# The MLP's second product as running PSUM sums over two pairs of output blocks, with the residual added by GpSimd's DMA in seven of eight groups

## The chip, the cores and the metric

One core of one Trainium2 chip. The metric is the device time of one execution in microseconds, the median of several runs; lower is better.

## The reference

Two residual layers over one sequence of 1024 positions, model width 1024, all in fp32. Layer 0 mixes tokens with a gated linear recurrence, layer 1 with causal attention ("fox"); beside each stands a cross-attention into 256 memory tokens ("kv" is its projection of the memory). Each layer ends in an MLP with squared ReLU:

```python
def sqrelu_mlp(h, w1, w2):
    return jnp.square(jax.nn.relu(h @ w1)) @ w2

for layer in range(DEPTH):            # DEPTH = 2
    h = rms_norm(x, norm_mix[layer])
    ...
    x = x + jnp.concatenate([y_mix, y_mem], axis=-1) @ w_out[layer]
    x = x + sqrelu_mlp(rms_norm(x, norm_mlp[layer]), w_mlp_in[layer], w_mlp_out[layer])
return x
```

`w_mlp_in` is 1024 x 4096, `w_mlp_out` 4096 x 1024.

## The kernel before

Activations stand transposed: 128 features on the partitions, 1024 positions in two halves of H = 512 columns. Each fp32 operand is split into a high and a low part in a rounded format (`r`, `wh`/`wl`), and a product is three matmuls (`t3`: high by high twice crossed with the low parts, summed in PSUM). The residual stream x lies in HBM as `xs` (the trace calls it xspill), in blocks of 128 features by 512 positions, 256 KB each.

The MLP (`mlp`) runs over eight groups g of four hidden blocks m = 4g to 4g+3. For each hidden block, `mlp_z` computes both halves of the first product, 24 matmuls for each into a bank of tag pj; VectorE takes the ReLU out of PSUM and GpSimd squares it. `hid_parts` makes the seven combinations of hidden blocks that a seven-product (Strassen-Winograd) 2x2 block multiplication needs, and splits them. `mlp_out` is the second product: 28 products of 6 matmuls, 168 per group. A group is 192 + 168 = 360 matmuls of 128x512, and the next group's first hidden block is computed ahead of the second product. The weights' own combinations are made by GpSimd in `_wsplit`, from raw loads into two `wraw` buffers.

In `mlp_out`, a step q works on a 2x2 group of blocks c11, c12, c21, c22: features 2q and 2q+1, both halves. Each of its seven products has its own PSUM bank. ScalarE copies the first out (L994), VectorE adds the others from PSUM into t, u or a residual block in SBUF (L995, L998, L1002, L1005, L1013, L1014, L1019, L1024: eight adds for each q), and GpSimd adds t and u into residual blocks (L1006, L1007, L1015). The four residual blocks are loaded by SyncE (`acc_load`, L449) and stored by it (`sink`, L980), in every group. In group 7 of layer 0, `sink` also adds the squares of the finished block to the sum for the next norm (`sqacc`, L398 to L407), and splits half 0's blocks as the next layer's input (L412, L413); the norm's matmuls (L341, into tag o, "pso") wait for the last of these sums. In group 7 of layer 1 it stores to the output.

The program is put in order by a scheduler that simulates the engines, so that instructions of neighbouring steps interleave on each engine; each engine then runs its own list in that order. SBUF blocks come from a pool of NU = 81 slots shared by all stages: a slot is written again when its earlier readers, DMAs among them, are done. PSUM has eight banks: two of tag pj, two of s, three of pt, one of o.

Of the kernel before, what the change touches and what calls it, by code (L numbers as in the profile page):

```python
# [19 lines left out]
P = 128  # L20
S = 1024
D = 1024
H = 512
# [133 lines left out]
class Builder:  # L157
    NU = 81
# [3 lines left out]
    def __init__(self, ctx, tc, ins, out):  # L162
# [13 lines left out]
        self.wraw = [cst.tile([P, 1056], F32, name=f"wr{i}") for i in range(2)]  # L176
# [23 lines left out]
        self.zz = {}  # L200
        self.xg = [None, None]
# [71 lines left out]
    def _wraw(self, upto):  # L273
        while self.wrawn < min(len(self.plan), upto):
            i = self.wrawn
            buf, src = self._wrawbuf(i), self.plan[i][0]
            n = 1024 if self.plan[i][2] == "s1" else self.plan[i][1]
# [9 lines left out]
    def _wsplit(self, upto):  # L287
        nc = self.nc
        while self.wload < min(len(self.plan), upto):
# [10 lines left out]
            elif parts in ("s1", "s2"):  # L300
                G, q = nc.gpsimd, 256
                a11, a12, a22, a21 = (raw[:, k * q:(k + 1) * q] for k in range(4))
                f = self.F.get()
                if parts == "s1":
                    self.wx = f
                    G.tensor_tensor(f[:, q:2 * q], a21, a22, ALU.add)  # L306
                    G.tensor_tensor(f[:, 0:q], f[:, q:2 * q], a11, ALU.subtract)  # L307
                    self._wpart(hi[:, 0:512], lo[:, 0:512], raw[:, 0:512], nc.vector)
                    self._wpart(hi[:, 512:1024], lo[:, 512:1024], f[:, 0:512], nc.vector)
                else:  # L310
                    G.tensor_tensor(f[:, 0:q], a11, a21, ALU.subtract)
                    G.tensor_tensor(f[:, q:2 * q], a12, self.wx[:, 0:q], ALU.subtract)
                    self._wpart(hi[:, 512:768], lo[:, 512:768], a22, nc.vector)
                    self._wpart(hi[:, 0:512], lo[:, 0:512], f[:, 0:512], nc.vector)
                    self.F.put(self.wx, f)
# [7 lines left out]
            self._wraw(self.wload + 2)  # L323

# [630 lines left out]
    def acc_load(self, q):  # L955
        return {(a, b): self.load_x(2 * q + a, b, self.xs) for a in range(2) for b in range(2)}

    def mlp_out(self, l, g, parts, acc):
        nc = self.nc
        V, G = nc.vector, nc.gpsimd  # L960
        n = slice(0, H)

        def prod(ps, blk, w, key):
            terms = []
            for p in range(2):
                c = slice(blk * M + p * P, blk * M + (p + 1) * P)
                terms += self.t3(w[0][:, c], w[1][:, c], *parts[p][key])
            for j, (a, b) in enumerate(terms):
                nc.tensor.matmul(ps, lhsT=a, rhs=b, start=(j == 0), stop=(j == 5))  # L969
            if q == 3:  # L970
                for p in range(2):
                    self.R.put(*parts[p][key])

        def sink(a, b):
            f = acc[(a, b)]
# [5 lines left out]
            if g == 7 and l == 0:  # L981
                self.sqacc(dm, b, x, V if b == 0 and a == 1 else None)
                if b == 0:
                    self.xg[0].append(self.split(x, self.pc("gmix1", dm)))
            self.F.put(f)

        for q in range(4):
            c11, c12, c21, c22 = (acc[(a, b)][:, n] for a in range(2) for b in range(2))
            w = self.wnext()
            tf, uf = self.F.get(), self.F.get()  # L990
            t, u = tf[:, n], uf[:, n]
            p1 = self.psum("pj")
            prod(p1, 0, w, "b11")
            nc.scalar.activation(t, p1, AF.Copy)  # L994
            V.tensor_tensor(c11, c11, p1, ALU.add)  # L995
            p2 = self.psum("pj")
            prod(p2, 1, w, "b21")
            V.tensor_tensor(c11, c11, p2, ALU.add)  # L998
            sink(0, 0)
            p6 = self.psum("pt")  # L1000
            prod(p6, 2, w, "t2")
            V.tensor_tensor(t, t, p6, ALU.add)  # L1002
            p5 = self.psum("s")
            prod(p5, 3, w, "t1")
            V.tensor_tensor(u, t, p5, ALU.add)  # L1005
            G.tensor_tensor(c12, c12, u, ALU.add)  # L1006
            G.tensor_tensor(c22, c22, u, ALU.add)  # L1007
            self.F.put(uf)
            nxt = self.acc_load(q + 1) if q < 3 else None
            w = self.wnext()  # L1010
            p7 = self.psum("s")
            prod(p7, 0, w, "t3")
            V.tensor_tensor(t, t, p7, ALU.add)  # L1013
            V.tensor_tensor(c22, c22, p7, ALU.add)  # L1014
            G.tensor_tensor(c21, c21, t, ALU.add)  # L1015
            self.F.put(tf)
            p3 = self.psum("pt")
            prod(p3, 1, w, "b22")
            V.tensor_tensor(c12, c12, p3, ALU.add)  # L1019
            sink(0, 1)  # L1020
            sink(1, 1)
            p4 = self.psum("pt")
            prod(p4, 2, w, "t4")
            V.tensor_tensor(c21, c21, p4, ALU.add)  # L1024
            sink(1, 0)
            acc = nxt

    def mlp(self, l, src, nz, nw, nxt=None):
# [11 lines left out]
        for g in range(8):  # L1040
# [6 lines left out]
            acc = self.acc_load(0)  # L1047
# [538 lines left out]
```

## Time and profile before

| | |
|---|---|
| median of 3 runs | 2181.33 us (2180.13 to 2185.57) |
| span of the profiled execution | 2182.0 us |
| mean granted TensorE clock | 0.992 |
| MLP of layer 0, steady groups | about 375 to 975 us |
| MLP of layer 1, steady groups | about 1650 to 2100 us |
| last matmul starts | 2175.14 us |

The engines are TensorE (PE), VectorE (DVE), ScalarE (ACT), GpSimd (POOL) and SyncE (SP), which issues most DMAs. A row of the groups of instructions reads: line, engine, operation, output tile, input tiles, shape, how often, busy us and mean ns of one, idle time before it and what ended that. "SPq" and "POOLq" are the queues of DMAs that SyncE and GpSimd issue.

### The profile page before, as it was taken

The numbers are of one execution on the slowest core, as the hardware profiler recorded it, in microseconds if no ns is written. First come the engines' busy times: TensorE is split into PE (matmuls) and PEld (weight loads), VectorE is DVE, ScalarE is ACT, GpSimd is POOL, SyncE is SP. The second block draws the span as 40 slices with busy tenths as digits, with TensorE's granted clock in tenths as the row PEclk, the third lists the DMA queues.
The fourth block names the chain that finished last, engine by engine and source line by source line (L and its number), as shares of the span: only waits on it lengthen the run. The fifth ranks groups of instructions, "written<-read, shape, count | busy, mean of one in ns | idle before, by whom it ended". The sixth has DMA issues, their size and how long they took to land. (4 is left out here: it accounts for less than half of the span.)

```text
span 2182.0 us, 31206 instructions
## 1 busy us (share of the span) xinstructions
PE 2124.3 (97%) x10662; PEld 1775.0 (81%) x10662; DVE 1621.9 (74%) x2942; ACT 906.4 (42%) x1776; POOL 944.4 (43%) x965
## 2 busy tenths in 40 slices
PE   8999999999999999998999999999999999999998
PEld 6898777888888888876999998776778888888887
DVE  8998685767767667779677778777887677677676
ACT  6755643232222222245555746656332322222322
POOL 3222312554544444448342324332555545545454
PEclk9999999999999999999999999999999999999999
DMA  5333253535435436444768446835365355354353
GB/s 184 126 88 90 90 189 108 178 115 174 157 116 191 145 112 202 136 154 155 262 243 288 139 145 204 280 91 152 114 214 177 109 163 163 119 182 147 114 191 132
DMA packets 152607, 345.71 MB, mean 158 GB/s; under 512 B 17088, under 2 KB 19200, under 8 KB 152448
## 3 DMA queue, kind: packets, MB, share of 16 engines
q1 hardware_dynamic: 143232, 318.49, 45.1%
q0 software_dynamic: 9216, 25.24, 3.8%
q8 instruction: 84, 1.38, 0.3%
q14 instruction: 75, 0.61, 0.1%
HBM read 237.65 MB, written 106.00 MB: 157 GB/s over the span
## 5 line engine op out<-in xcount | busy, mean ns | idle before, releaser
L348 PE MATMUL pspj<-r,wh 128*128 128x512 f32 x2576 | 818.6, 398 | 12.4 <-ACT wh L284 6.5
L348 PEld LDWEIGHTS pspj<-r,wh 128*128 128x128 f32 x2576 | 483.1, 189 | 125.1 <-ACT wh L284 6.9
L348 PE MATMUL pspj<-r,wl 128*128 128x512 f32 x1288 | 513.7, 399 | 2.0 <-DMA wl<-wsp 1.5
L284 ACT ACTIVATE wh<-wr 128x256 fp32r<-128x256 f32 (+3 forms) x417 | 242.5, 605 | 451.2 <-PE pspt L969 188.2
L285 DVE TENSOR_TENSOR wl<-wr,wh 128x256 fp32r<-128x256 f32 (+2 forms) x368 | 311.0, 853 | 85.2 <-ACT wh L284 84.4
L348 PEld LDWEIGHTS pspj<-r,wl 128*128 128x128 f32 x1288 | 245.9, 191 | 62.9 <-DMA wl<-wsp 2.8
L927 POOL TENSOR_TENSOR f<-f 128x512 f32<-128x512 f32 x128 | 153.5, 1199 | 325.3 <-DVE f L926 310.3
L348 PE MATMUL pspj<-wh,r 128*128 128x256 f32 (+1 forms) x1408 | 272.9, 288 | 8.0 <-ACT f L499 3.9
L418 ACT ACTIVATE r<-f 128x512 fp32r<-128x512 f32 x250 | 156.5, 630 | 293.3 <-POOL f L927 145.2
L421 DVE TENSOR_TENSOR r<-f,r 128x512 fp32r<-128x512 f32 x250 | 203.7, 826 | 74.0 <-ACT r L418 73.8
L969 PE MATMUL pspt<-r,wh 128*128 128x512 f32 x768 | 246.4, 395 | 1.0 <-DVE f L1019 1.0
L348 PEld LDWEIGHTS pspj<-wh,r 128*128 128x128 f32 x1408 | 223.8, 191 | 11.2 <-ACT f L499 4.4
L348 PE MATMUL pspj<-wl,r 128*128 128x256 f32 (+1 forms) x704 | 200.5, 285 | 0.9 <-DVE wl L285 0.9
L1006 POOL TENSOR_TENSOR f<-f,f 128x512 f32<-128x512 f32 x64 | 84.2, 1316 | 236.6 <-DVE f L1005 233.0
L969 PEld LDWEIGHTS pspt<-r,wh 128*128 128x128 f32 x768 | 143.7, 188 | 35.3 <-issue 2.1
L969 PE MATMUL pss<-r,wh 128*128 128x512 f32 x512 | 161.0, 395 | 3.6 <-ACT wh L284 2.7
L969 PE MATMUL pspj<-r,wh 128*128 128x512 f32 x512 | 160.1, 394 | 1.4 <-DVE f L995 1.4
L284 ACT ACTIVATE wh<-f 128x512 fp32r<-128x512 f32 x128 | 80.9, 632 | 180.5 <-PE pspj L969 76.5
L969 PE MATMUL pspt<-r,wl 128*128 128x512 f32 x384 | 151.8, 396 | 0.0
L926 DVE SCALAR_TENSOR_TENSOR f<-pspj,f 128x512 f32<-128x512 f32 x128 | 87.9, 688 | 77.2 <-PE pspj L348 72.8
L348 PEld LDWEIGHTS pspj<-wl,r 128*128 128x128 f32 x704 | 134.2, 191 | 2.3 <-DVE wl L285 1.3
L969 PEld LDWEIGHTS pss<-r,wh 128*128 128x128 f32 x512 | 95.9, 188 | 26.6 <-ACT wh L284 3.2
(279 smaller groups left out, 3647.7 us busy)
## 6 DMA issues: line engine op xcount, KB each, us to landing
f<-xspill SPq DMA_DIRECT2D x312, 256.0 KB, 3.3
xspill<-f SPq DMA_DIRECT2D x288, 256.0 KB, 3.3
wr<-in_w_dram SPq DMA_DIRECT2D x134, 512.0 KB, 3.9
f<-in_xT_dram SPq DMA_DIRECT2D x32, 256.0 KB, 3.9
wr<-in_wkv_dram SPq DMA_DIRECT2D x16, 512.0 KB, 3.7
wr<-in_wina_dram SPq DMA_DIRECT2D x15, 512.0 KB, 3.8
wsp<-wh SPq DMA_DIRECT2D x14, 512.0 KB, 4.5
wsp<-wl SPq DMA_DIRECT2D x14, 512.0 KB, 4.7
```

The source lines that it names most:

```text
L284: self.wact = self.nc.scalar.activation(hi, raw, AF.Copy)
L285: eng.tensor_tensor(lo, raw, hi.bitcast(F32), ALU.subtract)
L348: self.lastmm = self.nc.tensor.matmul(out, lhsT=a, rhs=b, start=(j == 0), stop=(j == n - 1))
L418: i = self.nc.scalar.activation(hi[:, :n], src, AF.Copy)
L421: self.nc.vector.tensor_tensor(lo[:, :n], src, hi[:, :n].bitcast(F32), ALU.subtract)
L926: nc.vector.scalar_tensor_tensor(r[:, n], ps, 0.0, self.rsb[h][:, n], ALU.max, ALU.mult)
L927: nc.gpsimd.tensor_tensor(r[:, n], r[:, n], r[:, n], ALU.mult)
L969: nc.tensor.matmul(ps, lhsT=a, rhs=b, start=(j == 0), stop=(j == 5))
L1006: G.tensor_tensor(c12, c12, u, ALU.add)
```

## The change

The second product is computed for two steps q at once (a pair u of q = 2u and 2u+1), in seven phases b11, b21, t2, t3, t1, t4, b22 of 2 x 6 matmuls. The products b11, t2, t1 and b22 are summed one after another in the same bank, one bank for each q of the pair: tag s for u = 0, tag pj for u = 1. ScalarE copies that running sum out after b11, after t2 and after t1. So a sum that VectorE or GpSimd formed from copies is now formed in PSUM by TensorE; the number of matmuls stays 168 in a group.

In groups 0 to 6 (`out_added`) no residual block is loaded: what a group adds to each block is made in an SBUF buffer, and GpSimd issues a DMA that adds it to the block in HBM (`send`, 16 in a group). Group 7 loads the blocks, adds to them in SBUF and stores them, since their values are needed for the norm or the output.

For this the weights come in another order, seven units of 1024 columns for a group; GpSimd combines them 512 columns at a time (L332 to L335), eight times in a group. There are three raw weight buffers in place of two, and two slots fewer in the pool.

```diff
-    NU = 81
+    NU = 79
...
-        self.wraw = [cst.tile([P, 1056], F32, name=f"wr{i}") for i in range(2)]
+        self.wraw = [cst.tile([P, 1056], F32, name=f"wr{i}") for i in range(3)]
...
+                    G.tensor_tensor(x["S3"][:, :512], a11, a21, ALU.subtract)
+                    G.tensor_tensor(x["S2"][:, :512], a22, x["S3"][:, :512], ALU.subtract)
+                    G.tensor_tensor(x["S1"][:, :512], a21, a22, ALU.add)
+                    G.tensor_tensor(x["S4"][:, :512], a12, x["S2"][:, :512], ALU.subtract)
...
-            for q in range(4):
-                self.plan += [(self.ins["w2"][(l * 8 + g) * 4 + q], 1024, "s1"), (None, 768, "s2")]
+            r = [self.ins["w2"][(l * 8 + g) * 4 + k] for k in range(4)]
+            self.plan += [(r[0], 1024, ("a11a12",)), (r[1], 1024, ("S2", "S3")), (None, 1024, ("S1", "a22")),
+                          (r[2], 1024, ("S4", "a11")), (r[3], 1024, ("a12", "S2")), (None, 1024, ("S3", "S1")),
+                          (None, 1024, ("a22", "S4"))]
...
     def mlp_out(self, l, g, parts, acc):
...
+        for u in range(2):
+            qs = (2 * u, 2 * u + 1)
+            ta, tc = ("s", "pt") if u == 0 else ("pj", "pt")
+            A = [self.psum(ta) for _ in qs]
...
+            def add_to(a, b, other=None):
+                def done(qq, q, ps):
+                    c = acc[(q, a, b)][:, n]
+                    V.tensor_tensor(c, c, ps, ALU.add)
+                    if other is not None:
+                        G.tensor_tensor(c, c, other[qq][:, n], ALU.add)
+                        self.F.put(other[qq])
+                        sink(q, a, b)
+                return done
+
+            if g < 7:
+                self.out_added(u, qs, A, t, t2, uu, phase, copy_to)
+                continue
...
+            phase(A, "b11", True, False, copy_to(t))
+            phase([self.psum(tc) for _ in qs], "b21", True, True, add_to(0, 0, t))
...
+            phase(A, "t2", False, False, copy_to(t2))
+            C = [self.psum(tc) for _ in qs]
+            phase(C, "t3", True, False, add_to(1, 1))
...
+            phase(A, "t1", False, False, mid)
...
+            phase(C, "t4", False, True, add_to(1, 0, t2))
...
+            phase(A, "b22", False, True, end)
+
+    def out_added(self, u, qs, A, t, t2, uu, phase, copy_to):
...
+        def send(f, q, a, b):
+            nc.gpsimd.dma_start(self.xs[2 * q + a, :, b * H:(b + 1) * H], f[:, n], accum_op=ALU.add)
+            self.F.put(f)
+
+        def plus(dst, a, b):
+            def done(qq, q, ps):
+                f = dst[qq][:, n]
+                V.tensor_tensor(f, f, ps, ALU.add)
+                if a is not None:
+                    send(dst[qq], q, a, b)
+            return done
+
+        phase(A, "b11", True, False, copy_to(t))
+        phase([self.psum("pt") for _ in qs], "b21", True, True, plus(t, 0, 0))
+        phase(A, "t2", False, False, copy_to(t2))
+        C = [self.psum("pt"), self.psum("o")]
+        phase(C, "t3", True, True, plus(t2, None, None))
...
+        phase(A, "t1", False, False, mid)
+        phase([self.psum("pt") for _ in qs], "t4", True, True, plus(t2, 1, 0))
...
+        phase(A, "b22", False, True, end)
```

Three places show how the order moves. First GpSimd's list in a steady group of layer 0, before; L306 to L312 combine weights (f is a slot, wr a raw buffer), L927 squares a hidden block, L1006 to L1015 add into the residual:

```order
L927 TENSOR_TENSOR f_479_4618<-f_479_4618 128x512
L311 TENSOR_TENSOR f_495_4765<-wr_72 128x256
L312 TENSOR_TENSOR f_495_4765<-wr_72,f_488_4711 128x256
L1006 TENSOR_TENSOR f_474_4552<-f_474_4552,f_482_4630 128x512
L1007 TENSOR_TENSOR f_476_4556<-f_476_4556,f_482_4630 128x512
L1015 TENSOR_TENSOR f_475_4554<-f_475_4554,f_481_4629 128x512
L306 TENSOR_TENSOR f_496_4801<-wr_71 128x256
L307 TENSOR_TENSOR f_496_4801<-f_496_4801,wr_71 128x256
L311 TENSOR_TENSOR f_503_4855<-wr_71 128x256
L312 TENSOR_TENSOR f_503_4855<-wr_71,f_496_4801 128x256
```

The same group in the change (L953 squares a hidden block, L1085 is the DMA that adds):

```order
L953 TENSOR_TENSOR f_449_4445<-f_449_4445 128x512
L335 TENSOR_TENSOR f_477_4631<-wr_73,f_475_4629 128x512
L334 TENSOR_TENSOR f_476_4630<-wr_71 128x512
L953 TENSOR_TENSOR f_468_4518<-f_468_4518 128x512
L953 TENSOR_TENSOR f_469_4546<-f_469_4546 128x512
L1085 DMA xspill<-f_470_4562 128x512
L1085 DMA xspill<-f_471_4570 128x512
L1085 DMA xspill<-f_472_4600 128x512
L1085 DMA xspill<-f_478_4644 128x512
L1085 DMA xspill<-f_473_4608 128x512
```

The combinations, which stood among the adds, now stand ahead of the second product among the squares; behind them stand the sixteen DMAs of the group, with no arithmetic between.

Second, VectorE's list at the end of layer 0's last group, before: adds from PSUM, low parts of weights (L285), splits of finished blocks (L413) and sums of squares (L407), which end with the sum that the norm waits for:

```order
L1005 TENSOR_TENSOR f_951_8908<-f_950_8907,pss_8942 128x512
L413 SCALAR_TENSOR_TENSOR r_954_8931<-f_940_8840,par,r_953_8930 128x512
L1024 TENSOR_TENSOR f_926_8734<-f_926_8734,pspt_8882 128x512
L407 TENSOR_TENSOR f_905_8597<-f_905_8597,f_947_8891 128x512
L413 SCALAR_TENSOR_TENSOR r_949_8895<-f_926_8734,par,r_948_8894 128x512
L285 TENSOR_TENSOR wl_77<-wr_71,wh_74 128x256
L1019 TENSOR_TENSOR f_941_8842<-f_941_8842,pspt_8971 128x512
L1013 TENSOR_TENSOR f_950_8907<-f_950_8907,pss_8961 128x512
```

And in the change (L1040 adds from PSUM, L286 makes low parts, L431 sums squares, L437 splits):

```order
L1040 TENSOR_TENSOR f_891_8372<-f_891_8372,pspt_8391 128x512
L387 SCALAR_TENSOR_TENSOR rmt_8700<-rmt_8700,vm_8697 128x2
L388 SCALAR_TENSOR_TENSOR rm_8699<-rmt_8700,rm_8699 128x2
L1040 TENSOR_TENSOR f_894_8415<-f_894_8415,pspj_8309 128x512
L286 TENSOR_TENSOR wl_79<-wr_73,wh_76 128x256
L1040 TENSOR_TENSOR f_895_8417<-f_895_8417,pspj_8310 128x512
L431 TENSOR_TENSOR f_850_8143<-f_850_8143,f_900_8463 128x512
L437 SCALAR_TENSOR_TENSOR r_902_8467<-f_890_8370,par,r_901_8466 128x512
L431 TENSOR_TENSOR f_850_8143<-f_850_8143,f_903_8479 128x512
```

Each q has four adds here where it had eight, the last four come as two pairs, and the small steps of the kv norm (L387, L388) stand among them.

Third, SyncE's list at the start of layer 1's MLP, before; L280 loads raw weights, L840 stores a residual block that the layer's output projection finished, L449 loads one and L980 stores one of the second product:

```order
L840 DMA xspill<-f_1640_15649 128x512
L280 DMA wr_72<-in_w_dram 128x1024
L840 DMA xspill<-f_1644_15676 128x512
L280 DMA wr_71<-in_w_dram 128x1024
...
L449 DMA f_1687_15990<-xspill 128x512
L980 DMA xspill<-f_1684_15984 128x512
L280 DMA wr_71<-in_w_dram 128x1024
L449 DMA f_1693_16073<-xspill 128x512
L980 DMA xspill<-f_1685_15986 128x512
```

In the change (L864 stores what the output projection finished, L281 loads raw weights):

```order
L864 DMA xspill<-f_1588_15154 128x512
L281 DMA wr_71<-in_w_dram 128x1024
L864 DMA xspill<-f_1592_15181 128x512
L281 DMA wr_72<-in_w_dram 128x1024
L281 DMA wr_73<-in_w_dram 128x1024
L281 DMA wr_71<-in_w_dram 128x1024
```

From the last store of the output projection on, only weight loads stand in the list until group 7.

More of the change, by code (lines that the diff above doesn't have):

```diff
@@ L299, in _wsplit @@
                     nc.gpsimd.dma_start(b, d[:, a:a + n])
[L300 to L315, printed above, removed]
+            elif isinstance(parts, tuple):
+                self._wunit(hi, lo, raw, parts)
             else:
@@ L961, in mlp_out, with prod, free, sink @@
         n = slice(0, H)
-        def prod(ps, blk, w, key):
+        seen = set()
+        def prod(ps, w, qq, key, start, last):
             terms = []
             for p in range(2):
-                c = slice(blk * M + p * P, blk * M + (p + 1) * P)
+                c = slice((qq * 2 + p) * P, (qq * 2 + p + 1) * P)
                 terms += self.t3(w[0][:, c], w[1][:, c], *parts[p][key])
             for j, (a, b) in enumerate(terms):
[L969 to L975, printed above, removed]
+                nc.tensor.matmul(ps, lhsT=a, rhs=b, start=(start and j == 0), stop=(j == 5), skip_group_check=not start)
+        def free(key):
+            for p in range(2):
+                self.R.put(*parts[p][key])
+        def sink(q, a, b):
+            f = acc.pop((q, a, b))
             x, dm = f[:, n], 2 * q + a
@@ L981, in sink @@
             if g == 7 and l == 0:
-                self.sqacc(dm, b, x, V if b == 0 and a == 1 else None)
+                self.sqacc(1 if b in seen else 0, b, x, V if b == 0 and a == 1 else None)
+                seen.add(b)
                 if b == 0:
-                    self.xg[0].append(self.split(x, self.pc("gmix1", dm)))
+                    self.xg[0][dm] = self.split(x, self.pc("gmix1", dm))
             self.F.put(f)
[L987 to L1026, printed above, removed]
@@ new lines, in mlp_out, with phase, copy_to, mid @@
+        for u in range(2):
+            qs = (2 * u, 2 * u + 1)
+            ta, tc = ("s", "pt") if u == 0 else ("pj", "pt")
+            A = [self.psum(ta) for _ in qs]
+            t, t2, uu = [None] * 2, [None] * 2, [None] * 2
+            def phase(banks, key, start, last, done):
+                w = self.wchunk()
+                for qq in range(2):
+                    prod(banks[qq], w, qq, key, start, last)
+                    done(qq, qs[qq], banks[qq])
+                if u == 1:
+                    free(key)
+            def copy_to(dst):
+                def done(qq, q, ps):
+                    dst[qq] = self.F.get()
+                    nc.scalar.activation(dst[qq][:, n], ps, AF.Copy)
+                return done
[11 more added lines that the diff above has]
+                continue
+            if u == 0:
+                self.acc_load(acc, u, 0, 0)
+            self.acc_load(acc, u, 1, 1)
+            phase(A, "b11", True, False, copy_to(t))
+            phase([self.psum(tc) for _ in qs], "b21", True, True, add_to(0, 0, t))
+            self.acc_load(acc, u, 1, 0)
+            phase(A, "t2", False, False, copy_to(t2))
+            C = [self.psum(tc) for _ in qs]
+            phase(C, "t3", True, False, add_to(1, 1))
+            self.acc_load(acc, u, 0, 1)
+            def mid(qq, q, ps):
+                copy_to(uu)(qq, q, ps)
+                c = acc[(q, 1, 1)][:, n]
+                G.tensor_tensor(c, c, uu[qq][:, n], ALU.add)
+                self.F.put(uu[qq])
+                sink(q, 1, 1)
+            phase(A, "t1", False, False, mid)
+            if u == 0:
+                self.acc_load(acc, 1, 0, 0)
+            phase(C, "t4", False, True, add_to(1, 0, t2))
+            def end(qq, q, ps):
+                add_to(0, 1)(qq, q, ps)
+                sink(q, 0, 1)
+            phase(A, "b22", False, True, end)
```

58 lines of the change are left out of this document (52 added, 6 removed).

## The prediction

> **What bounds the kernel now.** I read first the head of the page, then a table of busy time by stretch of 75 us, then the chain that ended last, then the waits of TensorE in the stretches that are not full.
>
> ```profile
> span 2182.0 us, 31206 instructions
> PE 2124.3 (97%) x10662; PEld 1775.0 (81%) x10662; DVE 1621.9 (74%) x2942; ACT 906.4 (42%) x1776; POOL 944.4 (43%) x965
> ```
>
> TensorE is busy 97% of the span, so at most 58 us could go without fewer matmuls, and the change has as many matmuls as before. The question is where those 58 us lie. The table by stretch has, for each engine, busy us and instructions in brackets, then the granted TensorE clock, the DMA share and GB/s:
>
> ```profile
> 675.00:750.00 75.00, 75.00 (x324) 60.69 (x323) 52.61 (x73) 22.28 (x35) 35.78 (x33) 1.00 0.45 142
> 975.00:1050.00 75.00, 63.99 (x361) 55.43 (x359) 70.51 (x136) 38.64 (x90) 53.56 (x49) 0.93 0.47 156
> 1500.00:1575.00 75.00, 72.13 (x308) 56.70 (x308) 56.76 (x83) 31.51 (x49) 28.62 (x32) 1.00 0.49 148
> 1575.00:1650.00 75.00, 71.53 (x305) 56.86 (x304) 59.53 (x78) 21.22 (x34) 43.55 (x38) 1.00 0.55 180
> 1650.00:1725.00 75.00, 75.00 (x323) 60.71 (x323) 53.02 (x75) 22.08 (x34) 35.93 (x31) 1.00 0.52 168
> 2025.00:2100.00 75.00, 75.00 (x323) 60.68 (x322) 51.17 (x75) 22.15 (x35) 35.22 (x34) 1.00 0.44 143
> ```
>
> In the MLP's steady groups (675, 1650, 2025) TensorE is busy 75.00 of 75.00, while VectorE has 22 us free and GpSimd 39. The two rows that matter are the others: 975–1050, where layer 0's last group runs into layer 1's start, lacks 11.0 us and has the clock at 0.93; and 1575–1650, layer 1's first group, lacks 3.5. The chain that ended last says the same of the steady groups:
>
> ```profile
> 1683.71 44.77 PE pspj L348 x192
> 1767.56 44.77 PE pspj L348 x192
> ```
>
> A group is 192 matmuls of the first product in 44.77 us, 0.233 each, and 168 of the second; it recurs every 1767.56 − 1683.71 = 83.85 us, which is 360 matmuls × 0.233. Nothing but matmuls is in it.
>
> **The change part by part.**
>
> *Groups 0 to 6.* Per group, VectorE's adds from PSUM go from 32 to 16, GpSimd loses 12 adds of 512 and 16 combinations of 256 and gets 8 of 512 and 16 DMA issues, ScalarE's copies go from 4 to 16, and SyncE loses 32 transfers. Prices:
>
> ```profile
> L998 DVE TENSOR_TENSOR f<-f,pspj 128x512 f32<-128x512 f32 x64 | 43.9, 687 | 39.2 <-PE pspj L969 36.5
> L1006 POOL TENSOR_TENSOR f<-f,f 128x512 f32<-128x512 f32 x64 | 84.2, 1316 | 236.6 <-DVE f L1005 233.0 <-issue 3.4
> L306 POOL TENSOR_TENSOR f<-wr 128x256 f32<-128x256 f32 x64 | 63.7, 995 | 122.0 <-DMA wr<-in_w_dram 71.3 <-DVE r L421 38.0 <-issue 6.1
> L299 POOL DMA_DIRECT2D wl<-wsp x32 | 17.9, 560 | 44.4 <-PE pspj L348 44.1 <-PE pspt L1257 0.2
> L994 ACT ACTIVATE f<-pspj 128x512 f32<-128x512 f32 x64 | 38.2, 597 | 62.7 <-PE pspj L969 58.8 <-DVE wl L285 3.8
> ```
>
> VectorE saves 16 × 0.687 = 11.0 us per group; GpSimd saves 12 × 1.316 + 16 × 0.995 = 31.7 and gets 16 × 0.560 for issues and 8 combinations of twice the width, about 8 × 1.5 by the 512-wide adds: 11 us less; ScalarE gets 12 × 0.597 = 7.2 us more on top of some 22 of 75. All of it lies beside matmuls that have no gap, so it is worth **nothing**: 14 groups × 0. Could it cost? A bank of running sums is copied out while TensorE writes other banks, and by the program's order comes back after 7 to 11 matmuls, 1.6 to 2.6 us; the copy is 0.60 us, so the cover is there two to four times over. If ScalarE were late by more than that, its lateness would be paid once per group.
>
> *The DMA that adds.* No row shows one. The nearest:
>
> ```profile
> xspill<-f SPq DMA_DIRECT2D x288, 256.0 KB, 3.3
> wl<-wsp POOLq DMA_DIRECT2D x16, 256.0 KB, 6.0
> wh<-wsp POOLq DMA_DIRECT2D x16, 256.0 KB, 5.1
> q1 hardware_dynamic: 143232, 318.49, 45.1%
> ```
>
> GpSimd's queue lands 256 KB in 5.1 to 6.0 us. These come in pairs, wh and then wl 0.56 us behind it, so the second lands 0.56 + 6.0 − 5.1 = 1.46 us after the first: a second transfer costs some 1.5 us of the queue, not 5. By the program's order the buffer sent is next written, at the closest, 96 matmuls after its send, 22.4 us, so a landing within 22.4 us costs nothing. The sends come in the second product, 16 in 39.1 us, one per 2.44 us. At c us per transfer in the queue the last lands about 16 × (c − 2.44) + 6 us after its issue: up to c = 3.5 nothing is paid. From below it could only help, and by nothing, since TensorE has no gap. I take **0**, and keep the other end as a rival.
>
> By the SyncE queue, 318.49 MB take 45.1% of 16 engines, 0.81 us for 256 KB. Per group, 32 × 0.81 = 26 us of all engines go and 16 × 0.81 = 13 come, so traffic isn't a limit. The Trainium skill (Collectives: The Full Stack, section "The bandwidth ceiling: the fold count and why AG ≠ RS ≠ AR") says that an add inside the DMA path is slow not for its arithmetic but because it reads two sources where a copy reads one. That speaks against the change: by it c would be an estimated 2 × 1.46 = 2.9 us, landings would stretch to some 13 us, and the sum would still stay as it is; no run here has shown it yet.
>
> *Layer 0's last group and the step to layer 1.* This group keeps loads and stores, but has 16 VectorE adds from PSUM where 32 stood, 12 GpSimd adds as before, and 12 ScalarE copies for 4. The waits of TensorE at 975–1045 (us in total, times, longest):
>
> ```profile
> PE pso L341 <- DVE f L407: 3.4, 1, 3.4
> PE pspj L348 <- ACT f L499: 2.2, 1, 2.2
> PE pspj L969 <- DVE wl L285: 1.1, 1, 1.1
> PE pspj L348 <- DVE f L998: 1.1, 1, 1.1
> PE pspt L969 <- DVE f L1019: 1.0, 1, 1.0
> PE pspj L348 <- DVE wl L285: 0.9, 2, 0.6
> PE pss L969 <- DVE f L1014: 0.9, 1, 0.9
> PE pspj L969 <- DVE f L995: 0.3, 1, 0.3
> ```
>
> They sum to 10.9 us, and all but 2.2 are waits for VectorE, which is busy 70.51 of 75: here, and only here, VectorE is the bound. The last ones in its line:
>
> ```profile
> 1031.05 0.68 DVE L1024 TENSOR_TENSOR f<-f,pspt 128x512 f32<-128x512 f32 x1
> 1032.42 0.69 DVE L407 TENSOR_TENSOR f<-f,f 128x512 f32<-128x512 f32 x1 [0.69 <-ACT f L401]
> 1033.17 1.87 PE L341 MATMUL pso<-cD,f 128*128 128x1 f32 x8 [3.40 <-DVE f L407]
> ```
>
> GpSimd's last sum of squares, and matmuls of the kv projection ahead of the norm and behind it:
>
> ```profile
> 1028.51 1.28 POOL L407 TENSOR_TENSOR f<-f,f 128x512 f32<-128x512 f32 x1
> 1027.12 0.40 PE L348 MATMUL pspj<-wh,r 128*128 128x256 f32 x2
> 1027.35 0.28 PE L348 MATMUL pspj<-wl,r 128*128 128x256 f32 x1
> 1035.47 0.63 PE L348 MATMUL pspj<-wh,r 128*128 128x256 f32 x2
> ```
>
> The last block's add (L1024) is followed by a square on ScalarE, the sum of squares L407, and the norm's matmuls. Sixteen adds fewer are 16 × 0.68 = **10.9 us** less in the queue that ends this chain. The waits say about the same: the short ones (1.1 + 1.1 + 1.0 + 0.9 + 0.9 + 0.3 = 5.3) and the 3.4 go, 8.7 us, and of the slow clock ((1 − 0.93) × 75 = 5.3 us) the half that follows the 3.4 us pause (two matmuls take 0.63 behind it, where they took 0.40), 2.6: 11.3. The bounds: all waits and all of the clock, 10.9 + 5.3 = 16; and what is left if another queue steps in. There are such queues. GpSimd has 53.56 of 75 and loses nothing here; its last sum of squares ended at 1028.51 + 1.28 = 1029.8, 3.4 us before the norm's matmuls began, so it alone would leave 3 to 4 us of gain. And the pairs' sums of the second pair hold both pj banks to the product's end, so the 40 or so kv matmuls that stood between the last products now stand behind them, and the first of those waits for an add that has 6 matmuls (1.4 us) of cover; I put 0.5 us on it. Between the last product and the norm 60 kv matmuls are left (7 us by (1027.35 − 1027.12) / 2 = 0.12 for one), and half 0's last block is now finished one phase, 12 matmuls, before the product ends. So what is late next should be GpSimd's sums of squares. I take **−10.9**, from −4 to −16.
>
> *Layer 1's first group.* The waits of TensorE at 1560–1640, and the pieces of the chain there:
>
> ```profile
> PE pss L969 <- ACT wh L284: 2.7, 1, 2.7
> PE pspj L969 <- DVE f L995: 1.0, 1, 1.0
> PE pspj L348 <- ACT r L418: 0.7, 1, 0.7
> ```
>
> ```profile
> 1591.53 2.50 DMA xspill<-f
> 1599.41 5.02 DMA wr<-in_w_dram
> ```
>
> The 2.7 us end with a weight split that waited for a weight load issued at 1599.41, late; SyncE stood in program order behind stores of residual blocks that waited for their sums. In the change no load or store of the accumulation stands in SyncE's order in this group, and a third raw buffer lets the load start one unit earlier. The 2.7 and the 0.7 should go: **−3.4**, from −4.4 (all three) to 0 (if 32 late loads of the fox stage's output product, which stay, hold it).
>
> *Two slots fewer, other stages.* The pool shrinks from 81 to 79 for the raw buffer. The mixer stages are made of chains, with TensorE at 72.13 of 75 in 1500–1575. The fewest free slots there, by the order of takes and returns, fall from 7 to 5, and reuse grows tighter. Bounds: below, the 2.9 us that this stretch lacks; above, as much again. I take **+1.5**, within ±5 for all such stages.
>
> *The tail.* After layer 1's last matmul stand one VectorE add and one store, in both: 0.
>
> Sum: −10.9 − 3.4 + 1.5 = −12.8 us on a span of 2182.0. The median of the runs, 2181.33, lies 0.7 below the span and inside the runs' own spread (2180.13 to 2185.57), so I take the sum from the median: 2168.5, **2169 us**.
>
> **The rivals.**
>
> *GpSimd takes VectorE's place at the layer step.* For it: 53.56 of 75, and nothing taken from it. Against: the blocks reach it earlier, since the adds ahead of them are halved. Then that term is −3.5, and the whole −3.5 − 3.4 + 1.5 = −5.4: 2176 us.
>
> *The work removed was hidden anyway, and the stages given fewer slots pay.* The gain at the step is that of the first rival or the forecast, the first group keeps its 2.7, and mixers pay 5 to 8: −2 on average, 2179 us.
>
> *All of the step goes.* −16 − 4.4 = −20.4 with the mixers at 0: 2161 us.
>
> *Slower: the adding DMA is too slow.* It decides at c = 3.5 us per 256 KB in GpSimd's queue. At c = 4 the last landing is 16 × 1.56 + 6 = 31 us after its issue, 8.6 beyond the 22.4 of cover, paid once a group: 14 × 8.6 = 120 us, less the 12.8: about 2289 us. For it: no row shows an add in the DMA path. Against it: 1.46 us per plain transfer, which would have to grow 2.4 times. The Trainium skill (SBUF — State Buffer, section "Who interferes with whom") has a rule that would feed it: VectorE holding the shared port starves GpSimd's writing of descriptors. The trace agrees only faintly, with minimum, median and maximum of an issue in ns at 527, 536 and 791 beside a VectorE three quarters busy:
>
> ```profile
> L299 POOL DMA_DIRECT2D wl<-wsp x32: 527/536/791, 1186.1 to 1510.8; - x32
> ```
>
>
> *It doesn't do what it says.* The program's order shows the sends and the missing loads, so I give this nothing.
>
> **How the numbers follow.** Forecast 0.47 (2163 to 2174); GpSimd steps in 0.19 (2172 to 2179); hidden and paid elsewhere 0.14 (2175 to 2186); all of it 0.11 (2157 to 2164); slower 0.09 (2190 to 2290). A measurement of this kernel can tell about 0.3% from no change, 6.5 us: faster is below 2174.8, slower above 2187.9. Faster: 0.47 + 0.11 + 0.05 of the second = 0.63. Within: 0.14 of the second and 0.11 of the third = 0.25. Slower: 0.09 and 0.03 of the third's far end = 0.12. The range takes in the unknown slots and the first, second and third rival, and leaves out the slow DMA and a little below: 2157 to 2187.
>
> **What would show it.** Right: steady stretches at 75.00 of 75.00 again with a period of 83.85 us; 975–1050 of the new profile with TensorE near 73 and the clock near 0.97, the 3.4 us wait for the sum of squares gone; landings of the adding DMA under 22 us. The first rival would show as waits for GpSimd in that stretch; the second as more waits around the fox stage; the slow DMA as TensorE, ScalarE or VectorE waiting for a DMA into the residual in every group. The prediction is wrong most easily if the scheduler's new order at the layer step puts a new chain there that no row of before shows.

## The result and the profile after

The change is **slower**, by some 1.1%: 2206.39 us median (2203.82 to 2207.87, 4 runs) against 2182.51 (2180.13 to 2185.57, 4 runs), a ratio of 1.0107, 95% interval 1.0095 to 1.0119. The forecast was 2169 us, from 2157 to 2187. The head of the page, its queues, and the rows of the DMAs that add:

```profile
span 2204.2 us, 30161 instructions
PE 2134.4 (97%) x10662; PEld 1777.7 (81%) x10662; DVE 1459.2 (66%) x2638; ACT 991.3 (45%) x1912; POOL 875.4 (40%) x893
q1 hardware_dynamic: 78720, 201.02, 28.1%
q0 software_dynamic: 41472, 83.97, 22.2%
L1085 POOL DMA_DIRECT2D xspill<-f x224 | 195.3, 925 | 361.2 <-DVE f L1091 297.5 <-ACT f L1034 60.5 <-issue 3.0
xspill<-f POOLq DMA_DIRECT2D x224, 256.0 KB, 5.4
```

VectorE lost 163 us of work and GpSimd 69, and the span grew by 22. The same stretches as before the change:

```profile
675.00:750.00 75.00, 74.19 (x319) 59.74 (x318) 43.13 (x57) 26.88 (x42) 33.44 (x29) 1.00 0.44 91
975.00:1050.00 75.00, 59.32 (x314) 49.84 (x312) 68.35 (x111) 42.34 (x95) 51.72 (x46) 0.91 0.43 141
1575.00:1650.00 75.00, 67.05 (x272) 52.25 (x271) 50.80 (x55) 26.32 (x42) 35.78 (x33) 0.95 0.58 120
1650.00:1725.00 75.00, 75.00 (x324) 60.80 (x323) 40.50 (x55) 27.09 (x44) 32.80 (x30) 1.00 0.56 106
2025.00:2100.00 75.00, 74.55 (x320) 59.98 (x320) 43.42 (x57) 25.46 (x39) 32.79 (x28) 1.00 0.47 94
```

The stretches of steady groups, full before, now lack 0.8, 0.0 and 0.5 us; the layer step lacks 15.7 where it lacked 11.0; layer 1's first group 8.0 where it lacked 3.5. To place every microsecond I take TensorE's **loss**: for each matmul the time from its start to the next start, less the pace of its shape when nothing waits (0.233 us for 128x512, 0.118 for 128x256, and so on). It holds the waits and also what matmuls take longer where the granted clock is below 1. Both programs have the same 10662 matmuls, so the losses of two stages can be compared however they shift:

| stage of the trace | before | change | difference |
|---|---|---|---|
| to layer 0's first second product | 31.7 | 29.4 | −2.3 |
| layer 0, groups 0 to 6 (up to matmul 4200) | −0.2 | 4.3 | +4.5 |
| layer step (matmuls 4200 to 5000) | 17.4 | 21.9 | +4.5 |
| matmuls 5000 to 7000 | 4.6 | 4.9 | +0.3 |
| fox stage (7000 to 7800) | 17.6 | 25.3 | +7.7 |
| layer 1, group 0 | 5.5 | 12.1 | +6.6 |
| layer 1, groups 1 to 6 | −0.2 | 3.1 | +3.3 |
| all matmuls | 79.0 | 102.6 | +23.6 |

(The rows leave out some short pieces between the stages; each column is one execution.) Five places lose, and in four of them the prediction had a gain or a zero.

### The profile page after: what moved, and what is told of

The parts are those of the page before. It is cut to its first block, busy times and chain, and to the rows that moved or that the text cites. A ratio compares the mean times of both kernels' runs of the same rounds, so it can differ in the third digit from the quotient of the medians.

```text
span 2204.2 us, 30161 instructions
## 1 busy us (share of the span) xinstructions
PE 2134.4 (97%) x10662; PEld 1777.7 (81%) x10662; DVE 1459.2 (66%) x2638; ACT 991.3 (45%) x1912; POOL 875.4 (40%) x893
## 3 DMA queue, kind: packets, MB, share of 16 engines
q0 software_dynamic: 41472, 83.97, 22.2%
## 5 line engine op out<-in xcount | busy, mean ns | idle before, releaser
L372 PE MATMUL pspj<-r,wh 128*128 128x512 f32 x2576 | 820.0, 398 | 17.9 <-DVE f L952 7.6
L286 DVE TENSOR_TENSOR wl<-wr,wh 128x1024 fp32r<-128x1024 f32 (+2 forms) x320 | 278.9, 883 | 116.3 <-ACT wh L285 115.8
L1085 POOL DMA_DIRECT2D xspill<-f x224 | 195.3, 925 | 361.2 <-DVE f L1091 297.5
L285 ACT ACTIVATE wh<-wr 128x256 fp32r<-128x256 f32 (+3 forms) x369 | 233.8, 658 | 208.7 <-PE pspj L372 81.0
L445 DVE TENSOR_TENSOR r<-f,r 128x512 fp32r<-128x512 f32 x250 | 217.7, 882 | 138.9 <-ACT r L442 138.0
L953 POOL TENSOR_TENSOR f<-f 128x512 f32<-128x512 f32 x128 | 183.0, 1433 | 208.4 <-DVE f L952 193.1
L997 PE MATMUL pspt<-r,wh 128*128 128x512 f32 x656 | 213.8, 400 | 4.8 <-ACT wh L285 3.1
L1091 DVE TENSOR_TENSOR f<-f,pspt 128x512 f32<-128x512 f32 x168 | 112.9, 686 | 134.2 <-PE pspt L997 83.3
L286 DVE TENSOR_TENSOR wl<-f,wh 128x512 fp32r<-128x512 f32 x128 | 107.9, 845 | 84.1 <-ACT wh L285 84.1
L997 PEld LDWEIGHTS pspt<-r,wh 128*128 128x128 f32 x656 | 124.8, 191 | 35.0 <-ACT wh L285 3.5
L997 PE MATMUL pspt<-r,wl 128*128 128x512 f32 x328 | 130.9, 400 | 1.2 <-DVE wl L286 1.2
L285 ACT ACTIVATE wh<-f 128x512 fp32r<-128x512 f32 x128 | 80.5, 631 | 112.6 <-PE pspj L372 73.0
```

What stands on the lines that cost most here:

```text
L285: self.wact = self.nc.scalar.activation(hi, raw, AF.Copy)
L286: eng.tensor_tensor(lo, raw, hi.bitcast(F32), ALU.subtract)
L372: self.lastmm = self.nc.tensor.matmul(out, lhsT=a, rhs=b, start=(j == 0), stop=(j == n - 1))
L445: self.nc.vector.tensor_tensor(lo[:, :n], src, hi[:, :n].bitcast(F32), ALU.subtract)
L953: nc.gpsimd.tensor_tensor(r[:, n], r[:, n], r[:, n], ALU.mult)
L997: nc.tensor.matmul(ps, lhsT=a, rhs=b, start=(start and j == 0), stop=(j == 5), skip_group_check=not start)
```

## The experiments

Each run is set against the kernel before on the same chip; the ratios have their 95% intervals. The median of the kernel before lay between 2182.42 and 2183.93 us in these sets, so a difference between two runs' medians is good to about 1.5 us. Where the recorded expectations give 10.6 or 10.7 us as the loss of layer 1's group 0, they divide the stages another way; by the table's division these are 12.1 and 9.8.

### Slots taken again too soon

The timeline of ScalarE in layer 1's group 0 of the change (start, us, instruction, in brackets the idle time ahead and its releaser) shows copies that wait for a DMA:

```profile
1588.45 0.60 ACT L1034 ACTIVATE f<-pss 128x512 f32<-128x512 f32 x1 [4.67 <-DMA xspill<-f]
1602.13 0.60 ACT L1034 ACTIVATE f<-pspj 128x512 f32<-128x512 f32 x1 [3.11 <-DMA xspill<-f]
1610.48 0.60 ACT L1034 ACTIVATE f<-pss 128x512 f32<-128x512 f32 x1 [6.10 <-DMA xspill<-f]
```

The answer for the source line of the adding DMAs says who waited for them (us, times), and how long they took to land:

```profile
  ACT f L1034: 17.6, 6
DMA to landing us min/median/max: 3.6/5.4/11.1
```

Copies out of the running sums wait for these DMAs, 17.6 us in six waits. The buffers are slots that such a DMA has not finished with: in the trace seven copies of this group, six of them after a wait, start 4.2 to 7.3 us (9 to 28 matmuls) after the issue of the DMA that sent their slot. They are no last reserve: at these takes 9 to 14 slots are free and 8 to 11 of them were given back earlier, but `Slots.get` (the pool's choice of a slot) adds a penalty of 100 returns to slots given back by the other instruction stream (here the fox stage), so it keeps going round the few, one to five, that the MLP has just given back.

```diff
     def mlp(self, l, src, nz, nw, nxt=None):
+        self.F.LATER = self.R.LATER = 0 if l else 100
```

> The change, with one number in the choice of a slot: in layer 1's MLP a slot given back by the side stream counts like any other (a penalty of 0, not 100 returns). In the change's first group of layer 1 the program takes slots that were sent 10 to 31 matmuls earlier (2.3 to 7.2 us), while eleven older ones lie free. Theory: the 10.6 us that the change loses in that group are waits for the adding DMA to land in slots taken again too soon. Then this run is 9 to 12 us faster than the change, about 2195 us, with no ScalarE copy waiting for a DMA into the residual there. Rival: that group is late because its weights are late (third raw buffer, new order of units); then it stays at 2206 within 2 us.

Measured: 2198.98 us (2198.09 to 2200.46), 1.0068 (1.0053 to 1.0083), 7.4 below the change. Group 0's loss fell from 12.1 to 6.3, and no copy there waits for a DMA any more. The theory holds, though with less than it expected: of the 12.1 us that the group lost, 5.8 go with the choice of slots. The rival (late weights) falls as the cause of these; what the remaining 6.3 are was not tested here.

The same line in the kernel before:

> The kernel before, with the slot penalty of 0 in layer 1's MLP. Its first group there has TensorE waits of 4.4 us and a chain with two stores of residual blocks that a later operation waited for. If these are slots taken again too soon, 2 to 4 us go, about 2179; if they are the late weight load, the time stays within 1 us of before.

Measured: 2178.96 us (2176.26 to 2186.04, 10 runs) against 2183.88, 0.9982 (0.9969 to 0.9996). The kernel before has the flaw too: its group 0 lost 2.8 in place of 5.5. This is the fastest of the kernels, with the one further below, and the fairer measure for any mended version of the change.

### Is it the adding DMA?

```diff
-            if g < 7:
+            if False:
                 self.out_added(u, qs, A, t, t2, uu, phase, copy_to)
```

> The change, with all eight groups on the path that loads the residual blocks, adds in SBUF and stores them (the path of group 7); no DMA adds. If the adding DMA is what makes the change slower, layer 1's first group gets back most of its 10.6 us and the time is 2190 to 2197 us; the steady groups would show whether their 0.6 us hang on the DMA as well. Rival: the running sums and the new weight order cost the time; then it stays at 2204 to 2210 us.

Measured: 2191.55 us (2187.37 to 2194.53), 1.0035 (1.0018 to 1.0053). The time is the one expected, but not from the place expected: group 0 of layer 1 still loses 9.8 (the change: 12.1), while the steady groups lose nothing at all (−0.5 and −0.4 us). So the steady loss comes only with the path that adds by DMA, and most of group 0's doesn't.

This edit and the slot rule together:

> No DMA adds (all groups load and store the residual blocks) and the slot penalty of 0 in layer 1's MLP. If the loss of 10.7 us that the run without DMA adds still has in layer 1's first group is the choice of slots too, it goes: 2182 to 2185 us, no slower than before by more than 0.2%. If the loss there is the new weight order or the running sums, it stays near 2191.

Measured: 2187.89 us (2185.34 to 2189.94), 1.0017 (1.0007 to 1.0026). Group 0 now loses 5.5, as in the kernel before: there it was the slots with plain loads and stores too. The time came out some 3 us above what was expected; what is left is mostly the fox stage, which loses some 10 us more than before.

### Why steady groups wait

The waits of TensorE in the change's steady groups of layer 0 (380 to 900 us):

```profile
PE pspj L372 <- DVE f L952: 3.2, 5, 0.9
```

```diff
-                    G.tensor_tensor(x["S3"][:, :512], a11, a21, ALU.subtract)
+                    V.tensor_tensor(x["S3"][:, :512], a11, a21, ALU.subtract)
...
-                    G.tensor_tensor(x["S1"][:, :512], a21, a22, ALU.add)
+                    V.tensor_tensor(x["S1"][:, :512], a21, a22, ALU.add)
```

> The change, with two of the four weight combinations of each unit pair (S3 and S1) on VectorE, not GpSimd. Theory: the 0.6 us that TensorE now waits once in nearly every steady group comes from four combinations that stand on GpSimd ahead of the squares; halved, the wait goes, 12 x 0.6 = 6 to 8 us less, about 2199 us. Rival: the wait comes from ScalarE's twelve added copies or from VectorE itself; then it stays or grows, 2206 or more.

Measured: 2207.79 us (2206.43 to 2210.65), 1.0109 (1.0094 to 1.0125): no gain, and the steady groups lose 4.8 us in layer 0 and 5.1 in layer 1, for 4.3 and 3.1. How many combinations GpSimd makes isn't the cause. The next theory was their order. GpSimd after one product of the change, then VectorE and TensorE:

```profile
430.45 0.86 POOL L1085 DMA_DIRECT2D xspill<-f  x1 [0.88 <-ACT f L1034]
438.73 1.29 POOL L332 TENSOR_TENSOR f<-wr,wr 128x512 f32<-128x512 f32 x1 [7.42 <-DMA wr<-in_w_dram]
439.99 1.28 POOL L334 TENSOR_TENSOR f<-wr 128x512 f32<-128x512 f32 x1
441.23 1.04 POOL L953 TENSOR_TENSOR f<-f 128x512 f32<-128x512 f32 x1
...
447.25 0.69 DVE L972 TENSOR_TENSOR f<-f,f 128x512 f32<-128x512 f32 x1 [0.93 <-POOL f L953]
...
450.86 0.69 DVE L952 SCALAR_TENSOR_TENSOR f<-pspj,f 128x512 f32<-128x512 f32 x1
...
451.60 0.73 PE L372 MATMUL pspj<-r,wh 128*128 128x512 f32 x2 [0.94 <-DVE f L952]
```

The same place without DMA adds:

```profile
435.20 1.04 POOL L953 TENSOR_TENSOR f<-f 128x512 f32<-128x512 f32 x1 [4.99 <-DVE f L952]
438.72 1.29 POOL L332 TENSOR_TENSOR f<-wr,wr 128x512 f32<-128x512 f32 x1 [2.48 <-DMA wr<-in_w_dram]
```

In both, L332 starts at 438.7, when the raw weights have landed. In the change L332 stands at the head of GpSimd's list and holds it for 7.4 us, and behind it waits a square (L953) that runs at 435.20 in the kernel without DMA adds. The square is late by some 6 us; VectorE's combinations of hidden blocks stand behind the squares, the next eviction L952 behind those, and TensorE waits 0.9 us for its bank. Why the scheduler put the combination first is not shown.

```diff
-            nc.gpsimd.tensor_tensor(r[:, n], r[:, n], r[:, n], ALU.mult)
+            if m % 4 == 1 and m > 4:
+                nc.scalar.activation(r[:, n], r[:, n], AF.Square)
+            else:
+                nc.gpsimd.tensor_tensor(r[:, n], r[:, n], r[:, n], ALU.mult)
```

> The change, with the squares of every group's second hidden block (m = 4g+1, from g = 1 on) on ScalarE, not GpSimd. Theory: the 0.6 us per steady group are GpSimd's order: a weight combination whose raw load hasn't landed stands ahead of these two squares, which are ready 4 to 6 us earlier, and VectorE's next evictions stand behind what needs the squares. With the squares on another engine no steady group has a wait of TensorE, and the time is 6 to 8 us below the change, about 2199 us. Rival: the DMAs that add slow the group in another way (their issue on GpSimd, 0.93 us each, or their traffic); then the steady waits stay near 0.6 us per group and the time near 2206.

Measured: 2191.49 us (2189.34 to 2198.32), 1.0042 (1.0025 to 1.0059), 14.9 below the change. Its steady stretches:

```profile
675.00:750.00 75.00, 75.00 (x324) 60.71 (x322) 45.21 (x59) 28.48 (x45) 32.63 (x29) 1.00 0.46 88
2025.00:2100.00 75.00, 75.00 (x324) 60.67 (x322) 45.82 (x59) 28.47 (x45) 32.41 (x29) 1.00 0.46 89
```

They are full again, with all DMA adds in place: the theory holds, and with the squares out of that list neither the issue of the adds nor their traffic costs a steady group anything. The gain is larger than expected, since group 0 of layer 1 loses 7.3 instead of 12.1 as well.

### The layer step

The waits of TensorE there in the change:

```profile
PE pspj L372 <- DVE f L1040: 7.0, 1, 7.0
PE pspj L997 <- ACT f L1034: 4.5, 1, 4.5
PE pspt L997 <- ACT r L442: 1.4, 1, 1.4
PE pspj L372 <- DVE r L593: 1.3, 1, 1.3
```

The 7.0 us are those before the first kv matmul, which waits for the last add from a pj bank. I had put 0.5 us on this wait. The 4.5 us end with a copy by ScalarE of a running sum, which itself waited for VectorE: it writes a slot that the splits for the kv projection (L549) were still reading.

```profile
990.20 0.60 ACT L1034 ACTIVATE f<-pspj 128x512 f32<-128x512 f32 x1 [4.04 <-DVE r L549]
```

On ScalarE's copies the prediction had said that lateness beyond their cover would be paid; it was, once, in this group.

```diff
-    "kvt": ('pt', 'pj'),
+    "kvt": ('pt', 's'),
```

> The change, with the kv projection of layer 1 in PSUM tag s, not pj. Theory: the 7.0 us that TensorE waits between layer 0's last product and the first kv matmul are there because both pj banks hold running sums to the end; with banks of their own the kv matmuls fill the gap, and this run is 5 to 8 us faster than the change, about 2200 us. Rival: VectorE's backlog sets the end of that stage whatever the banks are; then the wait moves to the norm's matmuls and the time stays within 2 us of 2206.

Measured: 2204.69 us (2202.59 to 2208.98), 1.0096 (1.0078 to 1.0114), 1.7 below the change and within the spread of both: the rival's case. The kv matmuls stand among the products again, and the step still loses 21.3 us (21.9): the 4.5 us stay, and the 7.0 are replaced by waits for weight parts, for the norm's sum and for kv evictions. A bank wasn't the limit.

VectorE's groups of instructions around the step, before (956 to 1050 us) and in the change (958 to 1055):

```profile
L421 DVE TENSOR_TENSOR r<-f,r 128x512 fp32r<-128x512 f32 x7 | 4.9, 719 | 0.7 <-ACT r L418 0.7
L285 DVE TENSOR_TENSOR wl<-f,wh 128x512 fp32r<-128x512 f32 x7 | 5.9, 847 | 0.0
```

```profile
L445 DVE TENSOR_TENSOR r<-f,r 128x512 fp32r<-128x512 f32 x8 | 8.9, 1117 | 2.5 <-ACT r L442 2.5
L286 DVE TENSOR_TENSOR wl<-f,wh 128x512 fp32r<-128x512 f32 x8 | 8.3, 1041 | 0.6 <-ACT wh L285 0.6
L1040 DVE TENSOR_TENSOR f<-f,pspt 128x512 f32<-128x512 f32 x12 | 8.1, 678 | 2.1 <-PE pspt L997 2.0
```

The adds from PSUM fell as forecast, 32 x 0.68 to 16 x 0.68 (twelve of them in the row above). But rows that read two operands from SBUF grew: the splits from 0.72 to 1.12 us, the weight parts from 0.85 to 1.04. Over all of VectorE's rows in these stretches (956 to 1050 and 958 to 1053 us), the changed number of instructions is worth −10.0 us and their changed length +10.0. The timeline of the change shows them with and without GpSimd beside them:

```profile
981.34 0.68 DVE L445 TENSOR_TENSOR r<-f,r 128x512 fp32r<-128x512 f32 x1
983.14 3.49 DVE L445 TENSOR_TENSOR r<-f,r 128x512 fp32r<-128x512 f32 x2
```

```profile
984.32 1.75 POOL L554 TENSOR_TENSOR f<-f,f 128x512 f32<-128x512 f32 x1
986.04 1.71 POOL L431 TENSOR_TENSOR f<-f,f 128x512 f32<-128x512 f32 x1
```

One split takes 0.68 us alone and 1.75 beside GpSimd's additions, which take 1.3 alone and 1.7 here. The Trainium skill (SBUF — State Buffer, section "Who interferes with whom") has the rule: a VectorE instruction with two inputs in SBUF and a GpSimd instruction that reads SBUF share one read interface. The trace agrees, and an add whose second operand is in PSUM stays at 0.68 us throughout. So the adds that the change removed were ones that no neighbour held up.

```diff
-                self.sqacc(1 if b in seen else 0, b, x, V if b == 0 and a == 1 else None)
+                self.sqacc(1 if b in seen else 0, b, x, V)
```

> The change, with the ten sums of squares that GpSimd makes in layer 0's last group on VectorE as well. Theory: at the layer step VectorE's operations with two operands in SBUF and GpSimd's arithmetic hold each other up (VectorE's splits took 1.12 us each there, against 0.72 before the change and 0.68 alone), so the 10.9 us of adds that went were given back in stretched rows. Taking 10 x 1.46 us from GpSimd for 10 x 0.68 on VectorE then shortens the stage: 3 to 6 us less than the change, about 2202, and the splits come back toward 0.7 us. Rival: VectorE is simply the longest queue; then ten more operations make it 5 to 8 us slower than the change.

Measured: 2198.14 us (2196.29 to 2202.80), 1.0069 (1.0052 to 1.0087), 8.2 below the change; the step's loss fell from 21.9 to 14.6, and the 7.0 us wait to 2.3. More work on the busiest engine made the stage shorter, so VectorE's count is not the bound. One sign of the theory failed: the splits stayed long (L445, 1176 ns), though other rows with operands in SBUF became shorter (L437 from 1203 to 1016 ns, L549 from 698 to 570). The run with two of the four weight combinations on VectorE points the same way: it lost 17.3 us at this step, for 21.9. That work taken from GpSimd shortens the step is shown; how the gain divides between the shared interface and GpSimd's in-order list stays open.

The same edit and the slot rule in the kernel before:

> The kernel before with the slot penalty of 0 in layer 1's MLP and the sums of squares of layer 0's last group all on VectorE. Moving those sums took 7 us from the layer step of the change (21.9 to 14.6 us beside TensorE's own pace between matmuls 4200 and 5000). If GpSimd and VectorE hold each other up there in the kernel before too, its 17.4 us fall by 2 to 5 and the time is about 2175, below both kernels. If the kernel before is bound by VectorE's count of operations there, the ten added ones make it 2 to 6 us slower than with the slot rule alone: 2181 to 2185.

Measured: 2178.93 us (2176.40 to 2182.79, 11 runs), 0.9979 (0.9970 to 0.9988): below before, and the same as with the slot rule alone. The step lost 16.7 for 17.4, with 6.8 us of waits for weight parts on VectorE in place of the wait for the norm's sum. Neither theory hit: moving the sums gives the kernel before nothing clear and costs it nothing.

### The memory of the change

```diff
-    NU = 81
+    NU = 79
...
-        self.wraw = [cst.tile([P, 1056], F32, name=f"wr{i}") for i in range(2)]
+        self.wraw = [cst.tile([P, 1056], F32, name=f"wr{i}") for i in range(3)]
```

> The kernel before with the memory of the change alone: 79 slots, three raw weight buffers. In all runs of the change, with or without DMA adds, TensorE loses about 25 us beside its own pace in the fox stage (matmuls 7000 to 7800 of 10662) where the kernel before loses 17.6. If that is the two slots that are gone, this run shows it there too: 24 to 26 us in that stage and 5 to 9 us over before in all, about 2190. If it comes from the change's weight order or products, which this run doesn't have, that stage stays at 17 to 19 us and the time within 2 us of before (a third raw buffer alone can only help).

Measured, for the kernel before with this alone: 2192.39 us (2188.94 to 2194.67), 1.0039 (1.0025 to 1.0054). The fox stage loses 26.2 us, where before lost 17.6 and the change 25.3. Its waits there (1340 to 1500 us), longest first, where the kernel before has 5.6 us in five waits, one wait of 2.1 and three of 0.4 or less:

```profile
PE pso L1247 <- ACT r L1260: 3.1, 4, 1.2
PE pss L1215 <- DVE mn L1220: 2.3, 5, 0.7
PE pso L1248 <- DVE r L1261: 1.7, 2, 1.2
PE pspj L348 <- DVE f L836: 1.7, 2, 1.2
```

So the fox stage's loss belongs to the memory and not to the second product. Among the kernels, one execution each, it varies: 17.6 to 19.8 us in the three kernels with the memory of before, 24.3 to 27.8 in those with the change's. Whether it is the two slots or the third buffer, which also reorders that stage, this run can't say.

### Mends together

The edits of the slot rule, of the squares and of the norm's sums, in one kernel:

> The change with three mends together: the slot penalty of 0 in layer 1's MLP, the squares of hidden block 4g+1 on ScalarE, the norm's sums on VectorE. Each alone gave 7, 15 and 8 us of the change's 2206; by stage they save 5.8 (first group of layer 1), 8.3 (steady groups) and 4 to 7 (layer step), 18 to 21 us together: 2185 to 2188, within 0.3% of before. What is then left over is the fox stage's 7 us.

Measured: 2182.50 us (2178.34 to 2189.24, 10 runs) against 2183.25, 1.0002 (0.9992 to 1.0012): the mends add up, to some 3 us more than expected, and the change is then level with the kernel before. The kernel before with the slot rule and the sums moved, on the same chip, is still 3.6 us faster (2178.93). The losses of the mended change: 28.6 to the first product, −0.5 and −0.5 in the steady groups, 15.2 at the layer step, 25.0 in the fox stage, 3.0 in group 0 of layer 1.

The last run gives the fox stage its 81 slots back. Its core, the choice of a raw buffer, where `"m"` marks the weights of the MLP's groups:

```diff
+            if self.plan[j][3:] == ("m",) and 2 not in self.rage:
+                self.rage.insert(0, 2)
...
+        if self.raw3 is None:
+            self.raw3 = (self.F.get(), self.F.get())
+        return Raw2(*self.raw3)
```

> The mended change (slot rule, squares of block 4g+1 on ScalarE, norm's sums on VectorE) with 81 slots and two raw buffers outside the MLP: the third raw buffer is borrowed from two slots while an MLP runs. If the two slots that are missing in the fox stage cost the 7 to 8 us that the memory of the change alone costs there, that stage falls from 25 to 17 to 19 us beside TensorE's own pace and the time is 2174 to 2177, below before by 0.3% and below the kernel before with the slot rule. If the loss in the fox stage hangs on something else (the third raw buffer's loads), it stays at 2181 to 2184.

Measured: 2183.76 us (2180.62 to 2186.20, 11 runs) against 2182.42, 1.0005 (0.9996 to 1.0014). A miss for the two slots, with the time that was expected for the other case: the fox stage lost 23.4, and the first mixer, which had lost 28.4 to 30.3 us in every run with the change's memory, went back to 32.2 (before: 31.7). The two slots alone don't explain the fox stage; the third buffer's part, or the order that the scheduler makes of either, stays open.

## Why the prediction was wrong, point by point

By place, the forecast of −12.8 us and the measured growth of 22 in the span differ by some 35; the places give nearly that: 15.4 at the layer step, 10.0 in layer 1's first group, 7.8 in the steady groups, 3.9 in the stages with fewer slots, less 1.4 at the tail.

**Steady groups: 0 forecast, +7.8 measured** (4.5 and 3.3). VectorE's count was right, it falls from some 53 to 43 of 75. GpSimd's was not: it falls from 36 to 33, some 3 us in a group for the 11 forecast. Of the 8 that are missing, 16 × (195.3 / 224 − 17.9 / 32) = 5.0 come from longer issues. The step that failed is "All of it lies beside matmuls that have no gap", with cover asked of ScalarE's copies alone. The question left out was what stands ahead of what in GpSimd's list; a combination that waits for a late load now stands ahead of a square. Shown by moving the squares, and by the run without DMA adds.

**The DMA that adds: 0 forecast.** The rival of a slow DMA did not come. Landings are 3.6, 5.4 and 11.1 us at the least, median and most. The software queue took (22.2% of 2204.2 − 3.8% of 2182.0) / 224 = 1.81 us of all 16 engines for one add of 256 KB, where the plain 256 KB takes 0.81: 2.2 times. The Trainium skill (Collectives: The Full Stack, section "The bandwidth ceiling: the fold count and why AG ≠ RS ≠ AR") says of the adds in its collectives that they read two sources where a copy reads one; the factor agrees with it. In the steady groups the doubling cost no time, as the run with squares on ScalarE shows.

**But the cover of 96 matmuls was wrong, and used for all fourteen groups.** With buffers matched between program and trace, 91 to 95 is about what ScalarE's copies have in a steady group; the first to write a sent buffer there is a weight combination on GpSimd (L335), some 66 matmuls or 15 us behind the send, which still covers the longest landing, 11.1. In layer 1's first group seven copies come 9 to 28 matmuls behind, 4.2 to 7.3 us with their waits, against landings of 5.4. The forecast there was −3.4, measured +6.6; 5.8 of the change's loss in that group go with the slot rule. The late weight load that I had followed was one of two causes at most: the kernel before, with the slot rule alone, already lost 2.8 for 5.5 there.

**The layer step: −10.9 forecast, +4.5 measured.** The step that failed is "Sixteen adds fewer are 16 × 0.68 = **10.9 us** less in the queue that ends this chain". The adds went; VectorE's busy time from the last group to the kv stage was 83.0 us in 94 before and 85.1 in 95 after, since other rows took longer (+10.0 us for −10.0). The upper rival ("GpSimd takes VectorE's place") pointed at the right engine but kept a gain of 3.5. The 0.5 us for the first kv matmul was mis-sized: 7.0; with banks of its own the loss only moved. The cover of ScalarE's copies, read as two to four times what is needed, failed once here, for 4.5 us.

**Two slots fewer: +1.5 forecast, +7.7 measured in the fox stage,** −2.3 in the first mixer. The mechanism had been named, with bounds of ±5 for all such stages; together they came to 5.4, at the edge of these, so the term was mis-sized. Shown to come with the memory by the kernel before; not resolved further.

**Tail: 0 forecast, −1.4 measured.** From the start of the last matmul to the end of the span it is 6.9 us before and 5.5 after; why is not shown.

**The rivals.** None was the case as a whole. The one on the slower side needed a slow DMA. The one in which stages with fewer slots pay 5 to 8 us had the size of the fox stage's loss, but kept a gain elsewhere. What happened were short waits in lists and slots, the longest of TensorE's at the layer step 7.0 us, with a growth of loss below 8 us in each of five places.

## What to carry to other kernels

Taking work off an engine that has spare time can lengthen the kernel through the order of what is left: read, for each in-order engine, what now stands at the head of its list and what it waits for, in every stage where a buffer is shared, and not in the steady one only. A cover read in a steady group is to be read again at each seam, where the pool has another history. Of adds that are removed, those with an operand in PSUM can relieve an engine by less than their count says, when its other work is held up by a neighbour.

## What the runs showed of the hardware that had not been expected

A DMA issue on GpSimd that adds takes it 863 ns in the median (854 at the least, 1505 at the most), where a plain one took 536. An add of 256 KB takes 1.81 us of the 16 DMA engines, a plain transfer 0.81, and still lands in 5.4 us. VectorE's split of 512 columns takes 0.68 us alone and 1.75 beside GpSimd's additions, while an add from PSUM stays between 0.67 and 0.69 in both; the small steps of a norm on two columns (128x2, 0.16 us alone) took up to 1.2 us there, as this row of the change shows:

```profile
1017.23 1.22 DVE L387 SCALAR_TENSOR_TENSOR rmt<-rmt,vm 128x2 f32<-128x2 f32 x1
```
